# Dilated attention in a decoder step: the statistics exchange moved to GpSimd's DMA queue, scaling of probabilities split from their transposes, and another trace order

## Chip, cores and metric

One core of one Trainium2 chip. The metric is the device time of one execution in microseconds (us), the median of several runs. Engines: PE (TensorE), DVE (VectorE), ACT (ScalarE), POOL (GpSimd) and SP, which here only issues DMAs.

## What is computed

One step of a two-layer decoder trunk for a prompt of 512 tokens and 8 samples of 4 tokens, all fp32: a recurrent block and a ConvFFN, then one shared K/V, then attention with its own queries, then a second ConvFFN. Only the attention is touched by the change. Cut to what matters:

```python
WINDOWS, DILATIONS = (128, 512, 2048), (1, 4, 16)      # three groups of queries, 8 heads of 64

def dilated_band_attn(q, k, v, dilation, span):        # one group; query t reads t, t-d, ..., t-window
    s = jnp.where(valid, einsum(q, k) * HEAD_DIM ** -0.5, -inf)
    m = max(s); p = exp(s - m); den = sum(p)
    return einsum(p, v) / den, m + log(den)

def combine_groups(outs, lses):                        # the three groups of a head are merged
    w = softmax(stack(lses), axis=0)
    return sum(w * stack(outs))
```

The prompt group and the sample group (whose keys are a cache of 256 rows and the 4 new ones) go through the same mathematics and share all weights.

## The kernel before, in words

All tokens are columns: 544 of them (512 prompt, 32 sample) in two halves of 272, features on the 128 partitions. Weights come from memory in units of 128x1024, and each is split by ACT and DVE (L132, L133) into two parts for three matmuls per product. The two FFNs, before and after the attention, take most of the time and are almost all matmuls.

**The attention** is the stretch between `man.close()` (L909) and `man.enter_context` (L1195). Outside it PE's order is that of the text. Inside it the tile framework's planner sets the order on every engine: it goes through the work by the order of the trace (what is written earlier has precedence) and takes what its own model of time holds to be ready. On the chip each engine, and each queue, then runs its list strictly in order. Some things so run earlier than they are written: the mask matmuls of `s_scores` for the first two samples stand between those of two heads.

For each of 8 heads `scores(h)` makes two blocks of scores in PSUM, one for the group of dilation 1 (L932, L937; queries in natural order) and one for the other two groups together (L949, L952; queries ordered by residue modulo 4). DVE takes the negative maximum of each row into `st` (L941, L956), ACT the exponentials into `P0` and `pt` with their sums into `st` (L945, L959), and POOL adds the two groups of `pt` into `P12` (L961). `pt` has two buffers. The P0 and P12 of heads 0 to 3 lie in the buffers that later take sample values; those of heads 4 to 7 use the 8 buffers of split weights.

Since the two blocks have their queries in different orders, the statistics of each must be brought into the order of the other before the groups can be merged. `exchange(half)` (L963) does it for four heads at once, through memory: two stores of 16 KB from `st` to `tok`, one for each block (L968, L969), and two loads from `tok` to `xt` (L970, L971), all four on SP's queue, each load behind the store of the same `tok`. `weights(half)` (L973) turns `st` and `xt` into the factors `sc` in eight small DVE operations and two of ACT (L978 to L987). `p_trans(h)` (L991) scales the head's probabilities by `sc` on DVE (L994, L996, L997), transposes them on PE (L1002, L1007) and moves the result from PSUM to `PT` with ACT (L1003) and DVE (L1008). `p_v(pair)` (L1018) multiplies two heads' `PT` by the values (L1034) and splits the result (L1038, L1039).

The samples run between the heads: `s_scores(b)` (L1062) for each of 8 batches, two at a time in `sample_pair`, in the two single PSUM banks, with keys `ck` loaded on SP's queue (L1048, 512 KB each, four buffers); `s_weights()` (L1076) merges their groups in a chain of small operations and ends with eight DVE scalings of `PS` (L1110); `s_values()` (L1112) transposes them (L1118), sums groups (L1121) and multiplies by the cached values (L1131). After the attention come the output projection (L194 with `OT`, then L1201) and the second FFN.

The order in which all this is written (L1149 to L1188) is in the code below.

Of the kernel before, what the change touches and what calls it, by code (L numbers as in the profile page):

```python
# [45 lines left out]
def trunk_kernel(ctx, tc, wall, xin, par_d, cst_d, msk_d, rope_d, bmask_d, ckT_d, cv_d,  # L46
                 y_d, h_d, conv_d, ffn_d, kT_d, v_d, vs_d):
    nc = tc.nc
    PE, ACT, DVE, POOL, SP = nc.tensor, nc.scalar, nc.vector, nc.gpsimd, nc.sync
# [30 lines left out]
    def big():  # L80
        return psum["pp"].tile([P, 2, 512], F32, name="big", tag="big")

    def bank():
        return psum["aux"].tile([P, 512], F32, name="bank", tag="bank")
# [826 lines left out]
    stat, P0, P12 = {}, {}, {}  # L911

    def own(i):

        return slice(0, 128) if i == 0 else slice(256 * i - 128, 256 * i + 128)
# [9 lines left out]
    def scores(h):  # L925

        c, kz = h // 2, KZ[h % 2][:, h // 2].rearrange("p (r j) -> p r j", r=4)
        half, hl = h // 4, h % 4
        st = stat[half][0]
        ps = big()  # L930
        for i in range(2):
            PE.matmul(ps[:, i, :], lhsT=identb, rhs=mskp[:, 512 * i:512 * i + 512], start=True, stop=True)  # L932
        for i in range(4):
            o = ps[:, i // 2, 256 * (i % 2):256 * (i % 2) + 256]
            for b in range(max(0, i - 1), i + 1):
                n = 128 * (b - i + 1)
                PE.matmul(o[:, n:n + 128].rearrange("p (r j) -> p r j", r=4),  # L937
                          lhsT=QT[0, c // 2][:, c % 2, 128 * i:128 * i + 128], rhs=kz[:, :, 32 * b:32 * b + 32],
                          start=False, stop=True, skip_group_check=True)
        pv_ = ps.rearrange("p x (y k) -> p (x y) k", k=256)  # L940
        DVE.tensor_reduce(st[:, 0, :, hl, 0], pv_, axis=AX.X, op=ALU.max, negate=True)  # L941
        P0[h], P12[h] = head_room(h)
        for i in range(4):
            lo = 128 if i == 0 else 0
            ACT.activation(P0[h][:, own(i)], pv_[:, i, lo:], AF.Exp, bias=st[:, 0, i, hl, 0:1],  # L945
                           accum_out=st[:, 0, i, hl, 1:2])
        ps = big()
        for i in range(2):
            PE.matmul(ps[:, i, :], lhsT=identb, rhs=msk[:, 1024:1536], start=True, stop=True)  # L949
        for r in range(4):  # L950
            for g in (1, 2):
                PE.matmul(ps[:, r // 2, 256 * (r % 2) + 128 * (g - 1):256 * (r % 2) + 128 * g],  # L952
                          lhsT=QT[g, c // 2][:, c % 2, 128 * r:128 * r + 128], rhs=kz[:, r], start=False, stop=True,
                          skip_group_check=True)
        pv_ = ps.rearrange("p x (y k) -> p (x y) k", k=256)
        DVE.tensor_reduce(st[:, 1, :, hl, 0], pv_, axis=AX.X, op=ALU.max, negate=True)  # L956
        pt = tp.tile([P, 4, 2, 128], F32, name="pt", tag="pt", bufs=2)
        for r in range(4):
            ACT.activation(pt[:, r].rearrange("p g k -> p (g k)"), pv_[:, r], AF.Exp, bias=st[:, 1, r, hl, 0:1],  # L959
                           accum_out=st[:, 1, r, hl, 1:2])  # L960
        POOL.tensor_tensor(P12[h], pt[:, :, 0], pt[:, :, 1], op=ALU.add)  # L961

    def exchange(half):  # L963
        st, xt, sc = stat[half]
        tok = [dram.tile([4, P, 8], F32, name=f"tok{half}{i}") for i in range(2)]

        flat = [t.rearrange("i p z -> (i p z)").rearrange("(j r z) -> j r z", r=4, z=8) for t in tok]
        SP.dma_start(tok[0].rearrange("i p z -> p i z"), st[:, 0].rearrange("p i e z -> p i (e z)"))  # L968
        SP.dma_start(flat[1], st[:, 1].rearrange("p r e z -> p r (e z)"))  # L969
        SP.dma_start(xt[:, 1].rearrange("p r e z -> p r (e z)"), flat[0])  # L970
        SP.dma_start(xt[:, 0].rearrange("p i e z -> p i (e z)"), tok[1].rearrange("i p z -> p i z"))  # L971

    def weights(half):  # L973
        st, xt, sc = stat[half]
        m1, m2, d1, d2 = st[:, :, :, :, 0], xt[:, :, :, :, 0], st[:, :, :, :, 1], xt[:, :, :, :, 1]
        t = [tp.tile([P, 2, 4, 4], F32, name=f"wt{i}", tag=f"wt{i}", bufs=1) for i in range(3)]

        DVE.tensor_tensor(t[0], m1, m2, op=ALU.min)  # L978
        DVE.tensor_tensor(t[1], t[0], m1, op=ALU.subtract)
        DVE.tensor_tensor(t[2], t[0], m2, op=ALU.subtract)  # L980
        ACT.activation(t[1], t[1], AF.Exp)
        ACT.activation(t[2], t[2], AF.Exp)
        DVE.tensor_tensor(t[0], t[1], d1, op=ALU.mult)
        DVE.tensor_tensor(t[2], t[2], d2, op=ALU.mult)
        DVE.tensor_tensor(t[0], t[0], t[2], op=ALU.add)
        DVE.reciprocal(t[0], t[0])
        DVE.tensor_tensor(sc, t[1], t[0], op=ALU.mult)  # L987

    PT = {}

    def p_trans(h, half, hl):  # L991
        sc = stat[half][2]
        p0, p12 = P0.pop(h), P12.pop(h)
        DVE.tensor_scalar(p0[:, own(0)], p0[:, own(0)], sc[:, 0, 0, hl:hl + 1], None, op0=ALU.mult)  # L994
        rest = p0[:, 128:896].rearrange("p (i k) -> p i k", k=256)
        DVE.tensor_tensor(rest, rest, sc[:, 0, 1:4, hl:hl + 1].to_broadcast([P, 3, 256]), op=ALU.mult)  # L996
        DVE.tensor_tensor(p12, p12, sc[:, 1, :, hl:hl + 1].to_broadcast([P, 4, 128]), op=ALU.mult)  # L997
        pt = tp.tile([P, 11, 128], F32, name="PT", tag="PT", bufs=2)
        PT[h] = pt
        ps = big()  # L1000
        for n in range(7):
            PE.transpose(ps[:, n // 4, 128 * (n % 4):128 * (n % 4) + 128], p0[:, 128 * n:128 * n + 128], ident)  # L1002
        ACT.activation(pt[:, 0:7].rearrange("p n q -> p (n q)"),  # L1003
                       ps.rearrange("p x y -> p (x y)")[:, 0:896], AF.Copy)
        ps = bank()
        for r in range(4):
            PE.transpose(ps[:, 128 * r:128 * r + 128], p12[:, r], ident)  # L1007
        DVE.tensor_copy(pt[:, 7:11].rearrange("p n q -> p (n q)"), ps)  # L1008
# [67 lines left out]
    def s_weights():  # L1076

        ps = bank()
        for i in range(2):
            PE.transpose(ps[0:8, 128 * i:128 * i + 128], sden[:, i], ident)  # L1080
        t = tp.tile([8, 2, 128], F32, name="sw", tag="pt", bufs=2)
        w = tp.tile([8, 128], F32, name="sw2")
        m = tp.tile([8, 3, 8, 4], F32, name="sw3")
        DVE.tensor_copy(t.rearrange("b i r -> b (i r)"), ps[0:8, 0:256])

        def by_group(x):
            return x.rearrange("b (h g s) -> b g h s", g=4, s=4)

        mm, dd, ww = by_group(t[:, 0]), by_group(t[:, 1]), by_group(w)
        POOL.memset(w, 0.0)  # L1090
        lo, acc, tt = (tp.tile([8, 8, 4], F32, name=f"sl{i}") for i in range(3))

        DVE.tensor_tensor(lo, mm[:, 0], mm[:, 1], op=ALU.min)
        DVE.tensor_tensor(lo, lo, mm[:, 2], op=ALU.min)
        for g in range(3):
            DVE.tensor_tensor(m[:, g], lo, mm[:, g], op=ALU.subtract)
        ACT.activation(m, m, AF.Exp)
        for g in range(3):
            DVE.tensor_tensor(acc if g == 0 else tt, m[:, g], dd[:, g], op=ALU.mult)
            if g:  # L1100
                DVE.tensor_tensor(acc, acc, tt, op=ALU.add)
        DVE.reciprocal(acc, acc)
        for g in range(3):
            DVE.tensor_tensor(ww[:, g], m[:, g], acc, op=ALU.mult)
        ps = bank()
        PE.transpose(ps[:, 0:8], w, ident[0:8, 0:8])
        wr = tp.tile([P, 8], F32, name="wr")
        DVE.tensor_copy(wr, ps[:, 0:8])
        for b in range(8):
            DVE.tensor_scalar(PS[:, b], PS[:, b], wr[:, b:b + 1], None, op0=ALU.mult)  # L1110

# [43 lines left out]
    def sample_pair(i):  # L1155
        for b in (2 * i, 2 * i + 1):
            s_scores(b)
            if b + 4 < 8:
                load_ck(b + 4)

    scores(4)
    sample_pair(0)
    weights(0)
    scores(5)
    sample_pair(1)
    for h in (0, 1):
        p_trans(h, 0, h)
        scores(6 + h)
    exchange(1)
    p_v(0)  # L1170
    sample_pair(2)
    p_trans(2, 0, 2)
    sample_pair(3)
    p_trans(3, 0, 3)
    for b in range(8):
        load_cv(b)
    s_weights()
    weights(1)
    p_v(1)
    p_trans(4, 1, 0)  # L1180
    p_trans(5, 1, 1)
    s_values()
    p_v(2)
    p_trans(6, 1, 2)
    p_trans(7, 1, 3)
    p_v(3)
    nxt["stop"] = firsts[1]
    conv_more(WBUFS - 2)  # L1188
# [195 lines left out]
```

## Time and profile before

| | us |
|---|---|
| median of 3 runs | 1279.61 (1278.06 to 1280.74) |
| the profiled execution, its own time | 1277.12 |
| its span, first to last instruction | 1275.2 |
| PE busy in the span | 1229.0 (96%) |
| DVE busy | 1035.0 (81%) |
| ACT busy | 701.4 (55%) |
| POOL busy | 175.6 (14%) |
| the attention, 739.6 to 834.9 | 95.3 |

The shares are over the whole span, where PE is almost never idle; the attention is the one longer stretch where it is, and where the clock that TensorE is granted falls. Times inside the span are given from its first instruction. A "releaser" in a row is the instruction that ended the engine's wait.

### The profile page before, as it was taken

What the parts mean: (1) busy time and instruction counts of PE and PEld (TensorE: products, weight loads), DVE (VectorE), ACT (ScalarE), POOL (GpSimd) and SP (SyncE); (2) the same over time, 40 slices, a digit from 0 to 9 for tenths busy, and PEclk for the clock granted to TensorE, in tenths of its full rate; (3) what the DMA queues carried; (4) which work ended last, traced back from release to release, by engine and by line L of the source; (5) the groups of instructions that cost most, each with busy time, mean ns of one, the idle gap of its engine ahead of it and who ended that gap; (6) DMA issues with size and microseconds to landing.
All of it is one profiled execution on the core that took longest, in us unless ns stands there. A gap on an engine that the chain in (4) does not pass through costs nothing.

```text
span 1275.2 us, 23856 instructions
## 1 busy us (share of the span) xinstructions
PE 1229.0 (96%) x9665; PEld 1197.0 (94%) x9665; DVE 1035.0 (81%) x1634; ACT 701.4 (55%) x1203; POOL 175.6 (14%) x235
## 2 busy tenths in 40 slices
PE   7999998999999999999999998798999999999998
PEld 7999998999999999999999886588999999999998
DVE  8985769998989797967878746789898989797963
ACT  5778646655555554545555365256655555454641
POOL 2464332000000000005113421032000000000000
PEclk9999999999999999999999998899899999999999
DMA  5232221233323232323245374321233323232422
GB/s 211 84 110 92 85 84 46 83 104 100 100 84 103 97 100 83 124 85 135 86 145 149 94 228 135 117 67 37 80 100 102 112 85 100 84 115 84 123 69 85
DMA packets 42909, 130.96 MB, mean 103 GB/s; under 512 B 7952, under 2 KB 8464, under 8 KB 42672
## 3 DMA queue, kind: packets, MB, share of 16 engines
q1 hardware_dynamic: 42800, 129.44, 32.1%
q8 instruction: 76, 1.25, 0.4%
q14 instruction: 33, 0.27, 0.1%
HBM read 121.03 MB, written 8.39 MB: 101 GB/s over the span
## 4 chain that ended last, share of the span: by engine, by line
PE 82%; DVE 8%; ACT 5%; issue 2%; POOL 1%; DMA 0%; SPq 0%; POOLq 0%; DVEq 0%; ACTq 0%
PE big L194 37%; PE bank L497 36%; PE big L881 2%; PE big L952 1%; DVE w L133 1%; PE big L937 1%; PE big L1034 1%; DVE hl L255 1%; ACT w L132 1%; PE big L1002 1%; ACT KZ L843 1%; PE big L760 0%; PE bank L1131 0%; DMA raw<-in_wall 0%; PE bank L881 0%
## 5 line engine op out<-in xcount | busy, mean ns | idle before, releaser
L194 PE MATMUL big<-HH,w 128*128 128x272 f32 x1536 | 259.3, 289 | 0.5 <-ACT cr L613 0.5
L194 PE MATMUL big<-hh,w 128*128 128x272 f32 x1280 | 219.9, 290 | 7.4 <-ACT hh L254 6.0
L497 PE MATMUL bank<-hh,w 128*128 128x272 f32 x1056 | 221.2, 289 | 0.0
L194 PEld LDWEIGHTS big<-HH,w 128*128 128x128 f32 x1536 | 218.0, 188 | 2.2 <-DVE X L638 1.3
L194 PEld LDWEIGHTS big<-hh,w 128*128 128x128 f32 x1280 | 184.1, 190 | 8.1 <-ACT hh L254 6.0
L497 PEld LDWEIGHTS bank<-hh,w 128*128 128x128 f32 x1056 | 175.0, 190 | 0.0
L194 PE MATMUL big<-HL,w 128*128 128x272 f32 x768 | 159.2, 288 | 0.8 <-DVE HL L307 0.8
L132 ACT ACTIVATE w<-raw 128x1024 fp32r<-128x1024 f32 (+1 forms) x111 | 113.4, 1029 | 76.6 <-PE big L194 59.0
L497 PE MATMUL bank<-t12h,w 128*128 128x272 f32 x704 | 142.4, 292 | 10.6 <-ACT snap L502 10.6
L497 PE MATMUL bank<-hl,w 128*128 128x272 f32 x528 | 152.3, 289 | 0.0
L133 DVE TENSOR_TENSOR w<-raw,w 128x1024 fp32r<-128x1024 f32 (+1 forms) x111 | 141.4, 1277 | 10.7 <-ACT w L132 5.8
L497 PE MATMUL bank<-t34h,w 128*128 128x272 f32 x704 | 146.2, 287 | 0.0
L194 PE MATMUL big<-hl,w 128*128 128x272 f32 x640 | 134.0, 291 | 1.9 <-DVE hl L255 1.9
L164 ACT ACTIVATE w<-sum 128x1024 fp32r<-128x1024 f32 x88 | 93.1, 1058 | 71.9 <-PE big L194 35.3
L497 PEld LDWEIGHTS bank<-t12h,w 128*128 128x128 f32 x704 | 115.3, 192 | 11.0 <-ACT snap L502 11.0
L194 PEld LDWEIGHTS big<-HL,w 128*128 128x128 f32 x768 | 120.6, 188 | 1.2 <-DVE HL L307 1.2
L502 ACT ACTIVATE snap<-bank 128x272 f32<-128x272 f32 x176 | 69.4, 395 | 89.5 <-PE bank L497 84.4
L165 DVE TENSOR_TENSOR w<-sum,w 128x1024 fp32r<-128x1024 f32 x88 | 107.5, 1222 | 13.3 <-PE bank L497 9.7
L497 PEld LDWEIGHTS bank<-t34h,w 128*128 128x128 f32 x704 | 115.7, 188 | 0.0
L194 PEld LDWEIGHTS big<-hl,w 128*128 128x128 f32 x640 | 101.3, 190 | 2.9 <-DVE hl L255 2.9
L497 PE MATMUL bank<-t12l,w 128*128 128x272 f32 x352 | 102.2, 290 | 0.0
L497 PE MATMUL bank<-t34l,w 128*128 128x272 f32 x352 | 101.1, 287 | 0.0
(277 smaller groups left out, 2278.1 us busy)
## 6 DMA issues: line engine op xcount, KB each, us to landing
raw<-in_wall SPq DMA_DIRECT2D x193, 512.0 KB, 3.5
ck<-in_ckT SPq DMA_DIRECT2D x8, 512.0 KB, 7.3
X<-in_xin SPq DMA_DIRECT2D x8, 272.0 KB, 6.1
out_y<-X SPq DMA_DIRECT2D x8, 272.0 KB, 2.1
cv<-in_cv SPq DMA_DIRECT2D x8, 256.0 KB, 4.4
cvt<-in_cv SPq DMA_DIRECT2D x4, 512.0 KB, 5.0
raw<-in_wall SPq DMA_DIRECT2D x6, 256.0 KB, 5.2
out_kT<-KT SPq DMA_DIRECT2D x2, 544.0 KB, 4.6
```

Of the source, the lines that this page charges most:

```text
L132: ACT.activation(hi[:, c0:c1], st, AF.Copy)
L133: DVE.tensor_tensor(lo[:, c0:c1], st, hi[:, c0:c1].bitcast(F32), op=ALU.subtract)
L164: ACT.activation(hi, flat, AF.Copy)
L165: DVE.tensor_tensor(lo, flat, hi.bitcast(F32), op=ALU.subtract)
L194: PE.matmul(ps[:, h, :T], lhsT=w[wi], rhs=x[xi][:, h, :], start=first and wi == 0 and xi == 0, stop=last and wi == 1)
L255: DVE.scalar_tensor_tensor(lo, X[k], g, hi.bitcast(F32), op0=ALU.mult, op1=ALU.subtract)
L497: PE.matmul(dst, lhsT=w, rhs=form(n, k, xi), start=first and k == 0 and wi == 0 and xi == 0, stop=k == 3 and wi == 1, skip_group_check=True)
L502: ACT.activation(t, src, AF.Copy)
L843: ACT.activation(KZ[a][rows, 2 * i + cc].rearrange("p (r j) -> p r j", r=4), residues(KT[i][rows, cc, 0:512]), AF.Copy)
L881: PE.matmul(o, lhsT=l, rhs=w[wi][:, 512 * kk:512 * kk + 512], start=k == 0 and wi == 0 and xi == 0, stop=k == KC - 1 and wi == 1)
L937: PE.matmul(o[:, n:n + 128].rearrange("p (r j) -> p r j", r=4), lhsT=QT[0, c // 2][:, c % 2, 128 * i:128 * i + 128], rhs=kz[:, :, 32 * b:3 ...
L952: PE.matmul(ps[:, r // 2, 256 * (r % 2) + 128 * (g - 1):256 * (r % 2) + 128 * g], lhsT=QT[g, c // 2][:, c % 2, 128 * r:128 * r + 128], rhs ...
```

## The change

It has three parts, all in the attention. The four DMAs of `exchange` are issued by POOL in place of SP. `p_trans` is cut in two: `p_scale(h)` holds the three DVE scalings, `p_trans(h)` the transposes and copies; likewise the eight scalings at the end of `s_weights` become `s_scale`. And the order of the trace is new: `scores(5)` and then `weights(0)` and `p_scale(0)` stand before `sample_pair(1)`; for heads 0 and 1 the next head's scaling follows the transposes, ahead of the next scores; `weights(1)` and `p_scale(4)` stand before `s_weights`, `s_scale` after the transposes of head 5, and `s_values` after `p_v(2)` and the scaling of head 7. No arithmetic is added or taken away.

```diff
     def exchange(half):
...
-        SP.dma_start(tok[0].rearrange("i p z -> p i z"), st[:, 0].rearrange("p i e z -> p i (e z)"))
-        SP.dma_start(flat[1], st[:, 1].rearrange("p r e z -> p r (e z)"))
-        SP.dma_start(xt[:, 1].rearrange("p r e z -> p r (e z)"), flat[0])
-        SP.dma_start(xt[:, 0].rearrange("p i e z -> p i (e z)"), tok[1].rearrange("i p z -> p i z"))
+        POOL.dma_start(tok[0].rearrange("i p z -> p i z"), st[:, 0].rearrange("p i e z -> p i (e z)"))
+        POOL.dma_start(flat[1], st[:, 1].rearrange("p r e z -> p r (e z)"))
+        POOL.dma_start(xt[:, 1].rearrange("p r e z -> p r (e z)"), flat[0])
+        POOL.dma_start(xt[:, 0].rearrange("p i e z -> p i (e z)"), tok[1].rearrange("i p z -> p i z"))
...
-    def p_trans(h, half, hl):
-        sc = stat[half][2]
-        p0, p12 = P0.pop(h), P12.pop(h)
+    def p_scale(h, half, hl):
+        sc, p0, p12 = stat[half][2], P0[h], P12[h]
         DVE.tensor_scalar(p0[:, own(0)], p0[:, own(0)], sc[:, 0, 0, hl:hl + 1], None, op0=ALU.mult)
         rest = p0[:, 128:896].rearrange("p (i k) -> p i k", k=256)
         DVE.tensor_tensor(rest, rest, sc[:, 0, 1:4, hl:hl + 1].to_broadcast([P, 3, 256]), op=ALU.mult)
         DVE.tensor_tensor(p12, p12, sc[:, 1, :, hl:hl + 1].to_broadcast([P, 4, 128]), op=ALU.mult)
+
+    def p_trans(h):
+        p0, p12 = P0.pop(h), P12.pop(h)
...
         DVE.tensor_copy(wr, ps[:, 0:8])
+        return wr
+
+    def s_scale(wr):
         for b in range(8):
             DVE.tensor_scalar(PS[:, b], PS[:, b], wr[:, b:b + 1], None, op0=ALU.mult)
...
     scores(4)
     sample_pair(0)
+    scores(5)
     weights(0)
-    scores(5)
+    p_scale(0, 0, 0)
     sample_pair(1)
     for h in (0, 1):
-        p_trans(h, 0, h)
+        p_trans(h)
+        p_scale(h + 1, 0, h + 1)
         scores(6 + h)
     exchange(1)
     p_v(0)
     sample_pair(2)
-    p_trans(2, 0, 2)
+    p_trans(2)
+    p_scale(3, 0, 3)
     sample_pair(3)
-    p_trans(3, 0, 3)
+    p_trans(3)
     for b in range(8):
         load_cv(b)
-    s_weights()
     weights(1)
+    p_scale(4, 1, 0)
+    wr = s_weights()
+    p_scale(5, 1, 1)
     p_v(1)
-    p_trans(4, 1, 0)
-    p_trans(5, 1, 1)
+    p_trans(4)
+    p_trans(5)
+    s_scale(wr)
+    p_scale(6, 1, 2)
+    p_v(2)
+    p_scale(7, 1, 3)
     s_values()
-    p_v(2)
-    p_trans(6, 1, 2)
-    p_trans(7, 1, 3)
+    p_trans(6)
+    p_trans(7)
     p_v(3)
```

## Rows read from the trace of the kernel before

**Rows 1.** Windows: the attention cut by stage (first row: scores of heads 0 to 5; then the first gap, the slow restart, scores 6 and 7, the work up to the second gap, the second gap, and the samples' values), and all that follows it. Columns: the stretch and its length in us; busy us and instructions of PE, weight loads, DVE, ACT, POOL; granted clock of TensorE as a share of full speed; busy share of the DMA engines; GB/s.

```profile
739.60:767.30 27.70, 26.95 (x241) 24.47 (x241) 14.61 (x13) 21.62 (x91) 6.53 (x7) 1.00 0.71 234
767.30:776.00 8.70, 3.11 (x42) 1.57 (x38) 3.67 (x15) 4.31 (x18) 1.27 (x1) 0.62 0.75 216
776.00:779.20 3.20, 3.20 (x14) 2.62 (x15) 3.20 (x7) 0.63 (x1) 0.00 (x0) 0.50 0.20 81
779.20:788.70 9.50, 9.50 (x80) 8.91 (x79) 7.90 (x10) 5.60 (x23) 1.27 (x1) 0.98 0.35 112
788.70:801.00 12.30, 12.28 (x185) 9.47 (x184) 6.70 (x22) 7.99 (x27) 1.28 (x1) 1.00 0.55 173
801.00:813.00 12.00, 7.81 (x34) 6.08 (x36) 10.71 (x33) 4.32 (x5) 0.00 (x0) 0.61 0.27 93
813.00:822.50 9.50, 7.88 (x79) 5.88 (x76) 8.37 (x21) 2.46 (x3) 0.00 (x0) 0.96 0.43 122
834.90:1275.20 440.30, 429.57 (x3389) 427.85 (x3388) 367.52 (x573) 227.26 (x388) 19.44 (x18) 0.99 0.28 90
```

**Rows 2.** Timeline of the first gap: start us, us, engine, line, operation, out<-in, shapes, count, and in brackets the idle time before it with its releaser.

```profile
770.03 0.37 PE L1064 MATMUL bank<-msk,identb 128*128 128x256 bf16 x1 [2.70 <-ACT PS L1074]
...
773.09 0.46 DVE L1073 TENSOR_REDUCE sden<-bank 128x1 f32<-128x288 f32 x1 [1.02 <-PE bank L1071]
773.47 0.18 DVE L978 TENSOR_TENSOR wt<-st,xt 128x32 f32<-128x32 f32 x1
...
775.28 0.19 DVE L987 TENSOR_TENSOR sc<-wt,wt 128x32 f32<-128x32 f32 x1
775.58 0.29 DVE L994 TENSOR_SCALAR P<-P,sc 128x128 f32<-128x128 f32 x1
...
775.92 0.48 PE L1002 MATMUL big<-cst,P 128*128 128x128 f32 x1 [2.90 <-DVE P L994]
```

**Rows 3.** Timeline of SP's queue around the two exchanges: start us, time of the issue, line, DMA, count.

```profile
758.72 0.38 SPq L968 DMA_DIRECT2D tok<-st  x1
761.11 0.33 SPq L969 DMA_DIRECT2D tok<-st  x1
766.92 0.33 SPq L1048 DMA_DIRECT2D ck<-in_ckT  x1
767.34 0.38 SPq L970 DMA_DIRECT2D xt<-tok  x1
767.78 0.42 SPq L971 DMA_DIRECT2D xt<-tok  x1
...
792.07 0.32 SPq L969 DMA_DIRECT2D tok<-st  x1
792.48 0.88 SPq L1053 DMA_DIRECT2D cvt<-in_cv  x2
793.52 0.38 SPq L971 DMA_DIRECT2D xt<-tok  x1
```

**Rows 4.** DMA issues, each from a window that holds the issue alone: the second store and the loads of the first exchange (the last of these three rows is the median of its two loads), then the second store and the last load of the second exchange. Columns: DMA, queue, count, KB each, us from issue to landing.

```profile
tok<-st SPq DMA_DIRECT2D x1, 16.0 KB, 3.1
...
xt<-tok SPq DMA_DIRECT2D x1, 16.0 KB, 3.1
...
xt<-tok SPq DMA_DIRECT2D x2, 16.0 KB, 3.3
...
tok<-st SPq DMA_DIRECT2D x1, 16.0 KB, 1.4
...
xt<-tok SPq DMA_DIRECT2D x1, 16.0 KB, 5.1
```

**Rows 5.** Timeline of POOL in the attention: the addition of heads 3, 4 and 7, columns as in the timeline above.

```profile
761.16 1.26 POOL L961 TENSOR_TENSOR P<-pt 128x512 f32<-128x512 f32 x1 [2.94 <-ACT pt L959]
765.37 1.27 POOL L961 TENSOR_TENSOR P12w<-pt 128x512 f32<-128x512 f32 x1 [2.94 <-ACT pt L959]
...
792.12 1.28 POOL L961 TENSOR_TENSOR P12w<-pt 128x512 f32<-128x512 f32 x1 [3.88 <-ACT pt L959]
```

**Rows 6.** Timeline of DVE in the second gap, columns as above.

```profile
799.52 0.17 DVE L978 TENSOR_TENSOR wt<-st,xt 128x32 f32<-128x32 f32 x1
799.62 0.18 DVE L1093 TENSOR_TENSOR sl<-sw 8x32 f32<-8x32 f32 x1
...
801.64 0.69 DVE L1039 TENSOR_TENSOR OT<-big,OT 128x512 fp32r<-128x512 f32 x1 [0.17 <-ACT OT L1038]
...
802.56 0.28 DVE L994 TENSOR_SCALAR P0w<-P0w,sc 128x128 f32<-128x128 f32 x1
...
805.38 2.31 DVE L1110 TENSOR_SCALAR PS<-PS,wr 128x288 f32<-128x288 f32 x8
...
808.22 0.94 DVE L996 TENSOR_TENSOR P0w<-P0w,sc 128x768 f32<-128x768 f32 x1
```

**Rows 7.** Timeline of the stage after the attention: one DVE operation alone, and the same operation beside one of POOL, columns as above.

```profile
839.69 0.79 DVE L255 SCALAR_TENSOR_TENSOR hl<-X,par,hh 128x544 fp32r<-128x544 f32 x1 [0.82 <-ACT hh L254]
...
850.39 1.37 POOL L274 TENSOR_TENSOR ss<-ss,sqx 128x544 f32<-128x544 f32 x1 [0.93 <-ACT sqx L268]
850.47 1.88 DVE L255 SCALAR_TENSOR_TENSOR hl<-X,par,hh 128x544 fp32r<-128x544 f32 x1
```

## The prediction

> **What bounds the kernel now.** I read the windows by stage first. After the attention PE is busy 429.57 of 440.30 us at a clock of 0.99 [rows 1]: nothing there waits on what the change touches, so a microsecond taken from the attention should come off the end. Inside it, the first 27.7 us (scores of heads 0 to 5) are PE at full clock and so is the stretch from 788.7 to 801. Two stretches are not [rows 1]. From 767.3 to 776.0 PE is busy 3.11 of 8.70 us, at 0.62, and restarts at half clock: 776.0 to 779.2 is busy throughout at 0.50 (1.2 GHz, the lower of its two levels; 1.00 is 2.4). From 801 to 813 it is busy 7.81 of 12.00 at 0.61. I call them the first and the second gap. The second has a different bound from the first: DVE is busy there 10.71 of 12.00 us, and 8.37 of the 9.50 behind it, where in the first it is busy only 3.67 of 8.70.
>
> Then I read the timeline of the first gap [rows 2]. PE waits twice: 2.70 us for a PSUM bank, freed by ACT's exponential of a sample, and 2.90 us for the first scaled probabilities. Behind the second wait stands a DVE chain: sample maxima at 773.09, `weights(0)` from 773.47, `sc` at 775.28, scaling at 775.58, transposes at 775.92. From L978 to the scaling it takes 775.58 - 773.47 = 2.1 us. Was `weights(0)` held by its data or by DVE's list? SP's queue and the landings tell [rows 3, 4]: the stores went out at 758.72 and 761.11, the second landed 3.1 us later, at 764.2; but the loads stood behind a `ck` load that could only go at 766.92, so they were issued at 767.34 and 767.78. One took 3.1 us, and with a median of 3.3 the other took 3.5: the data were there at 771.3. The remaining 2.2 us, to 773.47, are DVE's list: the maxima of samples 2 and 3 came first.
>
> In the second exchange nothing blocks the queue. Its second store goes at 792.07, lands in 1.4, the load goes at 793.52 and takes 5.1 us behind two 512 KB loads of `cvt`: 798.6 [rows 3, 4]. `weights(1)` starts at 799.52 [rows 6].
>
> **Part 1, the exchange on POOL.** Arithmetic is the same; four SP issues of 0.32 to 0.42 us [rows 3] per exchange go, and four POOL issues come. No DMA of the trace before is issued by POOL, so a leg (issue to landing of one) is bounded by rows. Below: SP's fastest, 1.4 us [rows 4]; a leg may come out shorter than now, since it no longer shares a queue with the large loads. Above: SP's slowest, 5.1 us [rows 4], and one POOL instruction's length, 1.3 us [rows 5], for the issue: 6.4. I take L = 3.5, nearest to the legs of the first exchange (3.1, 3.1, 3.5), which ran beside other loads as these will.
>
> The exchange's end is two legs in a row, second store and its load. On POOL the second store stands behind the addition of the same exchange's last head, written before it and ready at the same time: 761.16 + 1.26 = 762.4, and 792.12 + 1.28 = 793.4 [rows 5]. So the data land at 762.4 + 2L = 769.4 in the first (771.3 now), and at 793.4 + 2L = 800.4 in the second (799.52 is when it is used now). The first gets earlier, the second later by 2L - 6.1 = 0.9 us.
>
> Behind a waiting load on POOL stand the additions of later heads. Head 4's is ready at 765.37 [rows 5] and could wait for the last load's store. `pt` has two buffers, so ACT would miss it only two heads on, in scores 6 after 779.2 [rows 1]: more than 13 us of slack. I cost it at nothing; a wait beyond that would stop ACT and then PE by the excess. SP loses a blocker; it bounds nothing here.
>
> **Part 2, order at the first gap.** `weights(0)` and `p_scale(0)` now precede the maxima of samples 2 and 3. With data at 769.4 the first scaled block is there at 769.4 + 2.1 + 0.3 = 771.8. PE meanwhile runs the second sample pair, from 770.03 as now, since its bank is freed by ACT, which the change does not touch; it ends at 773.0. The transposes follow with no wait: 2.9 us gained. PE then runs without a break from 770.03. Now it restarts at 775.92 and is granted 0.50 until 779.2, which costs 3.2 x (1 - 0.50) = 1.6 us [rows 1]; I take 1.1 of it as saved, as the sample pair is then the slow restart. First gap: -2.9 - 1.1 = -4.0. What is late next there is the bank, 2.7 us, which stays. The scalings one head ahead gain nothing by themselves: PE is busy 9.50 of 9.50 us in the scores behind it [rows 1].
>
> **Part 3, order at the second gap.** Now the chain of `weights(1)` is interleaved with that of `s_weights`, and an `OT` operation of 0.69 us gets in: from 799.52 to the scaling at 802.56 it takes 3.0 us against 2.1 in the first half [rows 2, 6]. Head 5's scaling stands behind eight sample scalings of 2.31 us and ends at 809.16 [rows 6]. With the new order the first costs 0.9 less and the second 2.3 less for PE's next transposes. But both move DVE's work and remove none, and DVE is busy 10.71 + 8.37 = 19.08 of 21.5 us here [rows 1]: only the 2.4 us of idle time can be closed. I take -2.0, with 0 as one end (DVE ends its list when it did) and -4 as the other (PE's slow clock is recovered too, 0.61 over 7.81 us).
>
> **Sum.** -4.0 + 0.9 - 2.0 = -5.1 us: the profiled execution of 1277.12 goes to 1272.0. It lies 2.5 below the median of the runs; the forecast is made for the median: 1279.61 - 5.1 = 1274.5.
>
> On one point the Trainium skill speaks against the change. The rows first: the same DVE operation takes 0.79 us alone and 1.88 beside one of POOL's [rows 7], so the two engines hold each other up. SBUF — State Buffer, section "SBUF: two separate sides", says that POOL's DMAs have descriptors written by GpSimd, which a DVE operation in a two-port mode locks out, so that a DMA of about 620 ns takes about 3100. No row here shows such a DMA; by that figure each leg would be some 2.5 us longer, an estimate, and with L = 6.0 the sum would be a loss. The Trainium skill's page DMA: Bandwidth & Descriptors, section "Anatomy of one DMA — SWDGE (gpsimd) path", has it the other way, about 2.0 us fixed and little for 16 KB: with L = 2.0 the second exchange would be 2.1 us early and the sum near -8, an estimate as well.
>
> **Rivals.**
> (a) Slower: POOL's legs are long, by its own issue or by DVE's work on the ports. Both exchanges pay twice per leg. The first gap's gain lasts while 762.4 + 2L is well before 773.47 and is a loss above L = 5.5; the second pays 2L - 6.1. At L = 4.9 the second pays 3.7 against about 1.7 and 2.0 gained: the point from which it decides. At L = 6.0 the first loses 0.9, the second 5.9, and 2.0 is gained: +4.8, 1284.4. For it: POOL's operations are stretched in rows 7's manner, and the second exchange has little slack, 799.52 - 798.6. Against it: around 761 to 770 DVE is half idle.
> (b) No change: L near 4.4, and DVE's list behind the second gap ends when it did. The first gap gives -2.2 - 0.9, the second +2.7 and 0: -0.4, about 1279. For it: DVE's 19.08 of 21.5 us.
> (c) More: L about 2.5, the own queue passing the large loads. The second exchange is 1.1 early, the order is worth its full 4, the first gap gives 5: -10, about 1269.5. For it: legs of 1.4 us without traffic [rows 4].
> (d) The planner doesn't give the order that is written, for instance puts the sample maxima ahead of `weights(0)` again. Then only the data's 0 to 2 us remain; with the second exchange +0.9 and order -1 that is within 1 us of now, and is counted with (b). Behind the attention its lists on DVE and ACT may also fall otherwise; PE's idle time there is 10.7 us of 440.3 [rows 1], and I allow 1 to 2 us either way.
>
> **How the numbers follow.** Chances: forecast (-3 to -8) 0.48, (c) 0.11, (b) and (d) 0.21, (a) 0.20. About 0.2%, 2.6 us, is what a measurement of this kernel can tell from no change. Faster by more: 0.57, from the forecast and (c) less a small edge; within: 0.23; slower by more: 0.20. The range runs from (c) with planner's luck, 1268, to (a) at its price, 1284.5; the likeliest case's own range is 1271.5 to 1277.
>
> **What would show it.** Right: in the first gap PE's 2.90 us before L1002 gone, and the transposes directly behind the second sample pair; `sc` of the first half before 773; legs of POOL of about 3.5 us; L996 of head 5 before the eight L1110; the clock at 1.0 some 4 us earlier; scores 7 ended by about 785. Wrong: POOL's DMAs landing after 5 us or more, `weights(1)` starting more than 3 us later against the end of scores 7 than now (799.52 - 788.7 = 10.8), DVE without idle time from `weights(1)` to the last L1121 and that stretch as long as before, or new idle time of PE after the attention.

## The result, and the profile after

The changed kernel takes 1285.59 us (median of 6 runs, 1282.94 to 1287.68) against 1279.60 for the kernel before (6 runs): a ratio of 1.0053, 95% interval 1.0042 to 1.0065. It is slower by some 6 us where 5.1 us less were forecast, and it lies above the range. The profiled execution takes 1284.72 us with a span of 1282.6; before it was 1277.12 and 1275.2, so the pair of traces below differs by 7.4 to 7.6 us.

The windows by stage of the changed kernel, cut as before [rows 1] in front and at its own waits behind (from 792.40: the second exchange, the second gap in two rows, the samples' values, and what follows the attention; columns as in rows 1):

```profile
767.30:776.00 8.70, 2.72 (x26) 1.70 (x23) 5.93 (x14) 3.35 (x14) 1.26 (x1) 0.81 0.33 121
776.00:779.20 3.20, 3.20 (x30) 2.38 (x26) 1.52 (x3) 1.45 (x3) 0.00 (x0) 0.50 0.52 160
...
792.40:804.40 12.00, 8.06 (x120) 5.71 (x110) 3.02 (x6) 4.46 (x11) 3.11 (x4) 0.96 0.81 265
804.40:817.90 13.50, 11.00 (x86) 8.69 (x88) 12.59 (x43) 3.90 (x7) 0.00 (x0) 0.78 0.01 3
817.90:827.36 9.46, 5.59 (x37) 3.40 (x38) 9.18 (x25) 3.29 (x4) 0.00 (x0) 0.82 0.30 91
827.36:841.44 14.08, 12.45 (x107) 5.49 (x107) 5.76 (x11) 2.27 (x4) 0.00 (x0) 0.88 0.17 52
841.44:1282.60 441.16, 429.67 (x3389) 427.95 (x3388) 366.95 (x573) 227.29 (x388) 19.42 (x18) 0.99 0.28 90
```

The first gap is as wide as it was: PE is busy 2.72 of 8.70 us (3.11 before), although DVE now has 5.93 us of work in it (3.67 before). From 792.40 to 804.40 PE loses 3.94 us, where before it was busy without a break up to 801 [rows 1], and in the row behind, DVE is busy 12.59 of 13.50 us. What follows the attention is not the cause: PE is busy there as long as before (429.67 against 429.57).

For a comparison over all kernels I take four marks from the timelines of PE and DVE, in us after the first score matmul of the attention (L932, at 739.61 before and 739.75 after): the first transposes of scaled probabilities; the end of scores 7; from there to the first L978 of `weights(1)`; and from that to the first matmul on `OT`.

| | first transposes | end of scores 7 | to `weights(1)` | to `OT` | span |
|---|---|---|---|---|---|
| before | 36.3 | 49.15 | 10.76 | 35.32 | 1275.2 |
| after | 33.9 | 49.36 | 15.31 | 36.95 | 1282.6 |

So in this pair of traces the first half gave nothing (+0.2), the second exchange cost 4.55, the stretch behind it 1.63, and 0.9 came behind the attention: 7.3.

**The first gap.** The timelines of PE, DVE and ACT there, after (the third and later columns as in rows 2):

```profile
772.93 0.37 PE L1066 MATMUL bank<-msk,identb 128*128 128x256 bf16 x1 [5.45 <-ACT PS L1076]
...
773.64 0.47 PE L1004 MATMUL big<-cst,P 128*128 128x128 f32 x1 [0.31 <-DVE P L993]
```

```profile
767.15 0.19 DVE L978 TENSOR_TENSOR wt<-st,xt 128x32 f32<-128x32 f32 x1 [1.75 <-DMA xt<-tok]
767.26 1.22 DVE L956 TENSOR_REDUCE st<-big 128x4 f32<-128x1024 f32 x1
768.39 0.18 DVE L979 TENSOR_TENSOR wt<-wt,st 128x32 f32<-128x32 f32 x1
...
770.65 1.24 DVE L983 TENSOR_TENSOR wt<-wt,st 128x32 f32<-128x32 f32 x1 [1.98 <-ACT wt L981]
771.81 0.44 DVE L1075 TENSOR_REDUCE sden<-bank 128x1 f32<-128x288 f32 x1
...
773.30 0.28 DVE L993 TENSOR_SCALAR P<-P,sc 128x128 f32<-128x128 f32 x1
```

```profile
770.38 0.24 ACT L981 ACTIVATE wt<-wt 128x32 f32<-128x32 f32 x1
...
772.28 0.50 ACT L1076 ACTIVATE PS<-bank,sden 128x288 f32<-128x288 f32 x1 [1.55 <-DVE sden L1075]
```

The wait before the scaled probabilities is down from 2.90 to 0.31 us, and the wait for the bank is up from 2.70 to 5.45 [rows 2]: 5.60 became 5.76. The data were there at 767.15. But L956, head 5's maxima, stands behind L978, ACT takes the two exponentials of `weights(0)` (L981) only after those of head 5, at 770.38, and the sample maxima, which free the bank, stand behind L983 of `weights(0)`: 771.81. L983 itself took 1.24 us beside POOL's addition for head 5 (770.58 to 771.84), where the same instruction of `weights(1)` takes 0.18 (805.46).

**The second exchange.** The queues of POOL and SP after, and the chain that ended last (start us, us, what):

```profile
762.52 0.57 POOL L969 DMA_DIRECT2D tok<-st  x1
763.09 0.56 POOL L970 DMA_DIRECT2D xt<-tok  x1
764.79 0.76 POOL L971 DMA_DIRECT2D xt<-tok  x1 [1.15 <-DMA tok<-st]
...
792.48 1.27 POOL L961 TENSOR_TENSOR P12w<-pt 128x512 f32<-128x512 f32 x1 [1.20 <-ACT pt L959]
793.71 0.57 POOL L969 DMA_DIRECT2D tok<-st  x1
794.28 0.55 POOL L970 DMA_DIRECT2D xt<-tok  x1
797.72 0.76 POOL L971 DMA_DIRECT2D xt<-tok  x1 [2.89 <-DMA tok<-st]
```

```profile
792.52 1.89 SPq L1055 DMA_DIRECT2D cvt<-in_cv  x2
794.58 0.33 SPq L1062 DMA_DIRECT2D cv<-in_cv  x1
796.72 1.19 SPq L1055 DMA_DIRECT2D cvt<-in_cv  x2
798.00 1.94 SPq L1062 DMA_DIRECT2D cv<-in_cv  x3
```

```profile
792.48 1.23 POOL P12w L961
793.71 3.73 DMA tok<-st
797.44 0.28 issue
797.72 6.58 DMA xt<-tok
804.42 0.20 DVE wt L978
```

How that reaches PE, in the timelines of DVE and PE after:

```profile
804.42 0.19 DVE L978 TENSOR_TENSOR wt<-st,xt 128x32 f32<-128x32 f32 x1 [6.28 <-DMA xt<-tok]
...
804.86 0.68 DVE L1010 COPY PT<-bank 128x512 f32<-128x512 f32 x1
```

```profile
805.60 1.97 PE L1036 MATMUL big<-PT,VP 128*64 128x128 f32 x14 [5.14 <-DVE PT L1010]
```

In the first exchange the legs are 2.3, 2.0, 2.0 and 2.2 us, and the data land 4.3 us earlier than before (767.0 against 771.3). In the second the two legs in a row are 3.73 and 6.58 us, and they are on the critical chain: DVE stands still for 6.28 us in front of L978, and the copy to `PT` behind it in DVE's list (L1010) keeps PE waiting for 5.14. On SP the second store had gone out at 792.07, ahead of the first `cvt` load at 792.48, and landed in 1.4 us [rows 3, 4]. On POOL nothing holds that order: the store goes at 793.71, when the loads of `cvt` have been under way for a microsecond. This is a reading of one pair of traces; the experiments try it.

### The profile page after: what moved, and what is told of

Same layout as the page of the kernel before. It is cut to its first block, busy times and chain, and to the rows that moved or that the text cites. A ratio compares the mean times of both kernels' runs of the same rounds, so it can differ in the third digit from the quotient of the medians.

```text
span 1282.6 us, 23859 instructions
## 1 busy us (share of the span) xinstructions
PE 1230.2 (96%) x9659; PEld 1196.3 (93%) x9665; DVE 1036.0 (81%) x1634; ACT 701.4 (55%) x1203; POOL 180.4 (14%) x243
## 4 chain that ended last, share of the span: by engine, by line
PE 80%; DVE 8%; ACT 6%; issue 2%; DMA 2%; POOL 1%; SPq 0%; POOLq 0%; DVEq 0%; ACTq 0%
PE big L194 37%; PE bank L497 36%; PE big L881 2%; DVE w L133 1%; ACT w L132 1%; DVE hl L255 1%; DMA xt<-tok 1%; PE bank L1136 1%; PE big L937 1%; PE big L952 1%; ACT KZ L843 1%; DMA X<-in_xin 0%; POOL ss L274 0%; PE big L760 0%; PE big L1036 0%
## 5 line engine op out<-in xcount | busy, mean ns | idle before, releaser
L497 PEld LDWEIGHTS bank<-t12h,w 128*128 128x128 f32 x704 | 115.3, 191 | 10.4 <-ACT snap L502 10.4
```

Source lines behind the costliest of these rows:

```text
L497: PE.matmul(dst, lhsT=w, rhs=form(n, k, xi), start=first and k == 0 and wi == 0 and xi == 0, stop=k == 3 and wi == 1, skip_group_check=True)
```

## The experiments

Ratios are against the kernel before on the same chip, with their 95% interval. Three theories stood to be told apart: the second exchange on POOL is the loss, the new order is, or both; and for the exchange, the large loads beside it against POOL and DVE in each other's way.

**Four mixtures of queue and order.** The first is the changed kernel with the exchange on SP, the second the kernel before with it on POOL, the third and fourth the changed kernel with one exchange on POOL alone.

```diff
# e1, from the changed kernel (four DMAs; e2 is the reverse, from the kernel before)
-        POOL.dma_start(tok[0].rearrange(...
+        SP.dma_start(tok[0].rearrange(...
# e3, from the changed kernel (four DMAs; e4 has SP if half == 0 else POOL)
+        Q = POOL if half == 0 else SP
-        POOL.dma_start(tok[0].rearrange(...
+        Q.dma_start(tok[0].rearrange(...
```

The new order alone, on SP:

> The changed kernel with the exchange back on SP: split and order alone. Theory A (the last leg of the second exchange, late on POOL, starts weights(1) 4.9 us later than before and costs just that): weights(1) starts within 1 us of 799.5 and the time is 1285.6 - 4.9 = 1280.7. Theory B (the new order costs, by DVE's list and PE's slow clock at its end; the queue is harmless): about 1285, with the stretch from weights(1) to the end of the attention 37 us as in the changed kernel, against 35.4 before.

Measured: 1280.42, ratio 1.0016 (1.0006 to 1.0027). To `weights(1)` 10.29 us, from there to `OT` 37.01 (35.32 before). The order itself costs, behind the second exchange.

POOL alone, in the old order:

> The kernel before with the exchange on POOL and nothing else. Theory A: 1279.6 + 4.9 = 1284.5, with the last leg of the second exchange at 5 us or more and weights(1) at about 804. Theory B: 1279 or less, since the first exchange lands some 4 us earlier.

Measured: 1281.74, 1.0029 (1.0020 to 1.0038). To `weights(1)` 15.97, legs of 4.71 and 6.27 us; to `OT` 34.27.

The first exchange on POOL, new order:

> The changed kernel with only the first exchange on POOL, the second on SP. Theory A: 1280.7, as with both on SP, if the first gap gains nothing from data that land 4 us earlier; if it gains the forecast 4 us after all, 1277. Theory B: 1285.

Measured: 1277.68, 0.9991 (0.9981 to 1.0001). On SP again, the second exchange's legs are 1.41 and 4.51 us, and `weights(1)` comes after 9.37. PE waits 5.55 us for the bank in the first gap, as in the changed kernel.

The second exchange on POOL, new order:

> The changed kernel with only the second exchange on POOL, the first on SP. Theory A: 1285 to 1286, as the changed kernel. Theory B: 1285 as well, but with weights(1) at 800 and the loss behind it. A third reading, that POOL's exchange costs in the first gap (PE's bank wait of 5.4 us in place of 2.7), expects about 1283.

Measured: 1285.09, 1.0053 (1.0037 to 1.0068), as the changed kernel; legs of 5.24 and 5.44.

What follows: the POOL queue is worth -2.7 us at the first exchange (1277.68 against 1280.42) and +4.7 at the second (1285.09 against 1280.42). With +2.0 of the order that makes +4.0, by medians of about a microsecond's uncertainty each; the changed kernel is at +6.0, so the parts don't add up. One reason shows: beside a second exchange on POOL, the first one on POOL gained nothing (1.0053 in the changed kernel, 1.0053 in e4), so the -2.7 can't be counted there. The order alone (+2.0, e1) and the queue alone (+3.3, e2: 1281.74 against 1278.41) make +5.3.

**The old order with the first exchange on POOL alone** (`Q = POOL if half == 0 else SP` in the kernel before):

> The kernel before, its order kept, with only the first exchange on POOL and the second on SP. If the first exchange's early data are worth what the run with POOL alone showed (scores 7 end 1.8 us earlier) and the second's landing on SP is as before, weights(1) starts some 1.8 us earlier and the time is 1278.4 - 1.8 = 1276.6 (before at 1278.4 on this kind of chip). If the whole gain needs the new order as well: 1278 to 1279.

Measured: 1276.44, 0.9980 (0.9972 to 0.9989). PE's two waits in the first gap became one:

```profile
770.85 0.45 PE L1003 MATMUL big<-cst,P 128*128 128x128 f32 x1 [3.84 <-DVE P L995]
```

3.84 in place of 5.60, 1.8 us less. The first transposes start 5.2 us earlier (31.1 after the first score matmul against 36.3), but scores 7 end only 1.0 us earlier: the second sample pair, which PE did in its gap before, is now behind the transposes.

**The changed kernel with the loads held.** A POOL write into each buffer, which needs the second exchange's data, stands before the loads of `cvt` and the late ones of `cv`, so that these start when the statistics have landed:

```diff
# e6, from the changed kernel (the same before the cv loads of b > 5)
+            POOL.tensor_copy(t[:, 0, 0:1], stat[1][1][:, 0, 0, 0, 0:1])
             SP.dma_start(t.rearrange("p c e -> p (c e)"), cv_d[b])
```

> The changed kernel, both exchanges on POOL, with the loads of cv that ran beside the second exchange held back until it has landed (POOL writes one element of each of their tiles from xt first; eight copies of one column). Theory A1 (the 512 and 256 KB loads in flight make the legs long): the second exchange's last legs fall from 3.7 and 6.6 us to 2.0 to 2.3, as in the first, weights(1) starts some 5 to 6 us after the end of the additions of head 7, and the time is 1285.6 - 5 = about 1280. Theory A2 (a POOL DMA is slow there for another reason, DVE's operations on the shared ports or POOL's own work): the legs stay at 4 us or more and the time at 1285.

Measured: 1277.73, 0.9993 (0.9984 to 1.0002), some 8 us below the changed kernel, and `weights(1)` after 8.95 us. Its DMA issues, window 790 to 806 (columns as in rows 4, each the median of two), and the windows over the two legs in it (first) and over the two legs in the changed kernel (second and third):

```profile
tok<-st POOLq DMA_DIRECT2D x2, 16.0 KB, 1.9
xt<-tok POOLq DMA_DIRECT2D x2, 16.0 KB, 2.1
```

```profile
794.41:798.73 4.32, 4.32 (x63) 3.22 (x61) 1.83 (x4) 2.80 (x6) 1.89 (x4) 1.00 0.09 11
```

```profile
793.71:797.44 3.73, 3.73 (x55) 2.77 (x53) 1.48 (x3) 2.33 (x5) 1.12 (x3) 1.00 0.84 269
797.72:804.42 6.70, 2.74 (x34) 1.77 (x30) 0.42 (x1) 0.77 (x4) 0.76 (x1) 0.93 0.89 300
```

With the DMA engines at 0.09 a leg on POOL takes 1.7 to 2.2 us, at 0.84 and 0.89 it takes 3.7 and 6.6. DVE speaks against the other theory: it is busier beside the short legs (1.83 of 4.32) than beside the longest (0.42 of 6.70). So it is the large loads.

**The fastest mixture of these parts**: old order, first exchange on POOL, second on SP, the large loads issued on SP behind its last DMA (`with tc.issue_after(last[1]):` around the loads of `cvt`, and of `cv` for b > 5; those of b = 4 and 5 behind the last `ck` load).

> The order of before, first exchange on POOL, second on SP with the loads of cv of samples 0 to 3 and 6, 7 issued behind its last load. Theory A1: that last leg falls from 4.5 to 5.1 us to 1.4 to 2.0, weights(1) can start 2 to 3 us earlier, 1276.6 - 2 = 1274.6; if DVE's and PE's lists hold weights(1) instead, no gain, 1276.6. Theory A2 expects the leg as it was.

Measured: 1275.55, 0.9982 (0.9973 to 0.9992); the two legs in a row of the second exchange are 1.4 and 1.9 us. Though they sum to 3.3 against 6.5 before, `weights(1)` is only 1.2 us earlier (9.54): DVE's list and PE's work in front of it are next. Against e5, 0.9 us are gained, less than the intervals can tell. In e5 the legs were 4.7 and 1.8, for there the planner put one `cvt` load ahead of the store on SP's own queue (L1054, L970), and two others behind the exchange's last load (L972):

```profile
791.07 0.33 SPq L1054 DMA_DIRECT2D cvt<-in_cv  x1
791.50 0.37 SPq L970 DMA_DIRECT2D tok<-st  x1
...
796.22 0.37 SPq L972 DMA_DIRECT2D xt<-tok  x1
796.68 0.93 SPq L1054 DMA_DIRECT2D cvt<-in_cv  x2
```

**The store ahead of the addition**: the changed kernel, with head 7's POOL addition put behind the exchange.

```diff
# e8
-        POOL.tensor_tensor(P12[h], pt[:, :, 0], pt[:, :, 1], op=ALU.add)
+        add = lambda: POOL.tensor_tensor(P12[h], pt[:, :, 0], pt[:, :, 1], op=ALU.add)
+        if h < 7: add()
+        else: late.append(add)
...
     exchange(1)
+    late.pop()()
```

> The changed kernel with POOL's addition of head 7 written behind the exchange, so that the second store need not stand behind it. If the 1.3 us of that addition, which let two large loads of cvt go out first, are what makes the second exchange late, its two legs become 2 and about 5 us, weights(1) starts some 3 us earlier and the time is about 1282.5. If only the 1.3 us themselves count: 1284.3. If the legs stay as they are whatever the start: 1285.6.

Measured: 1285.01, 1.0051 (1.0038 to 1.0064). The store goes 1.0 us earlier, at 792.69, still behind the first `cvt` load (792.52), takes 4.90, and the load goes at 797.88, as late as ever, and takes 5.8. A start 1.0 us earlier is worth nothing here. A store ahead of the large loads on POOL's queue was not tried, since this one still came behind the first of them.

**The order, one half at a time**, all exchanges on SP. e9 is the changed kernel with the second half's order of before, e10 that with the first half's:

```diff
# e9, from the changed kernel (beside SP in the exchange)
+    s_scale(s_weights())
     weights(1)
+    p_v(1)
     p_scale(4, 1, 0)
-    wr = s_weights()
...
-    s_scale(wr)
...
# e10, from the changed kernel (beside SP in the exchange)
-    scores(5)
     weights(0)
-    p_scale(0, 0, 0)
+    scores(5)
     sample_pair(1)
     for h in (0, 1):
+        p_scale(h, 0, h)
         p_trans(h)
-        p_scale(h + 1, 0, h + 1)
...
```

> All exchanges on SP. The first half's steps stand in the changed kernel's order (scaled probabilities and statistics as there, up to the transposes of head 3), the second half's in the order of before. Theory, the second half's order is what costs the 1.6 us that the run with the changed order on SP alone showed between the second weights and the outputs: here that stretch stays at 35.3 us as before, the first stretch at 33.7, and the time at about 1278.8, no change. Rival, the first half's order costs it (DVE enters the second half with its work in another sequence): the stretch is 37.0 us and the time about 1280.4.

Measured: 1277.88, 0.9998 (0.9987 to 1.0009), to `OT` 35.29.

> All exchanges on SP, the mirror of the run beside it: the first half in the order of before, the second half's weights, scaled probabilities and transposes in the changed kernel's order. Theory, the second half's order costs: the stretch from the second weights to the outputs is 37.0 us and the time about 1280.4 (ratio 1.0013). Rival, the first half's order costs: 35.3 us and about 1278.8.

Measured: 1280.33, 1.0018 (1.0009 to 1.0028). The second half's order is what costs. (Its stretch to `OT` is 41.2 us in a profiled execution that took 2.4 us more than the median; the excess is PE at half clock: the two groups of 16 value matmuls take 3.64 us each, 1.93 and 1.92 in e9.) The row that moved is `wr`, the sample weights, on which the eight sample scalings wait; `weights(1)` (first row) and `wr` of e9, then of e10:

```profile
799.76 0.17 DVE L978 TENSOR_TENSOR wt<-st,xt 128x32 f32<-128x32 f32 x1
...
805.35 0.17 DVE L1110 COPY wr<-bank 128x8 f32<-128x8 f32 x1 [0.30 <-PE bank L1108]
805.63 2.32 DVE L1115 TENSOR_SCALAR PS<-PS,wr 128x288 f32<-128x288 f32 x8
```

```profile
800.23 0.18 DVE L978 TENSOR_TENSOR wt<-st,xt 128x32 f32<-128x32 f32 x1
...
808.96 0.17 DVE L1110 COPY wr<-bank 128x8 f32<-128x8 f32 x1 [0.45 <-PE bank L1108]
810.00 0.69 DVE L1010 COPY PT<-bank 128x512 f32<-128x512 f32 x1 [0.88 <-PE bank L1009]
...
811.97 0.69 DVE L1010 COPY PT<-bank 128x512 f32<-128x512 f32 x1 [1.00 <-PE bank L1009]
812.58 2.03 DVE L1115 TENSOR_SCALAR PS<-PS,wr 128x288 f32<-128x288 f32 x7
```

`wr` comes 5.59 us after `weights(1)` in e9 and 8.73 in e10; the scalings end at 807.95 and at 814.61, and in e10 DVE stands idle three times in front of them (0.45 + 0.88 + 1.00).

**DVE's list, made shorter.** e11 is e7 with the eight sample scalings on ACT, e12 is e6 with the same edit:

```diff
-            DVE.tensor_scalar(PS[:, b], PS[:, b], wr[:, b:b + 1], None, op0=ALU.mult)
+            ACT.activation(PS[:, b], PS[:, b], AF.Copy, scale=wr[:, b:b + 1])
```

> The order of before, the first exchange on POOL, the second on SP with the big context loads held until its data have landed (the fastest kernel so far, 1275.55), and here the scaling of the eight score tiles of the second half is done by ACT in place of DVE. Theory, DVE's list of work bounds the stretch from the second weights to the outputs (12.59 of 13.50 us busy in the changed kernel): some 2.3 us come off DVE, the stretch falls from 34.2 to about 32, and the time to about 1273.3. Rival, the chain through the scaled probabilities, their transposes and the matmuls bounds it: the stretch stays at 34.2 and the time at 1275.5; if ACT becomes the bound instead, it grows to about 36 and the time to 1277.5.

Measured: 1271.46, 0.9943 (0.9931 to 0.9956): the fastest kernel here, 7 us below the kernel before on its chip. To `OT` 30.96 us. ACT takes 3.50 us for the eight, in its idle time:

```profile
804.02 3.50 ACT L1116 ACTIVATE PS<-PS,wr 128x288 f32<-128x288 f32 x8
```

> The changed kernel (new order in both halves, both exchanges on POOL) with the big context loads held until the second exchange has landed, and with the eight sample scalings of the second half done by ACT. Without the last it took 1277.73 us, ratio 0.9993. Theory, the new order costs because DVE waits for the sample weights with the eight scalings (2.31 us) still on its list: with these on ACT the order costs nothing, and the time comes to about 1272, as the run of the old order with the same edit (1271.46), the stretch from the second weights to the outputs to about 32 us. Rival, the order delays the sample scalings whoever does them, and the transposes behind them wait: about 1275, the stretch at 34 us or more.

Measured: 1274.22, 0.9966 (0.9954 to 0.9979), to `OT` 34.55. DVE's 2.3 us are worth 3.5 here (from 1277.73), but the rival was right on the order: it still costs 2.8 against e11, with the scalings off DVE. `wr` comes 10.33 us after `weights(1)` (808.50 - 798.17), 5.04 in e11 (802.87 - 797.83). (e11 also has its second exchange on SP, but `weights(1)` comes as long after scores 7 in both, 9.55 us in e11 and 9.45 here.) ACT waits for `wr`:

```profile
808.68 3.52 ACT L1118 ACTIVATE PS<-PS,wr 128x288 f32<-128x288 f32 x8 [3.11 <-DVE wr L1113]
```

## Why the prediction was wrong

**What bounds the kernel.** The two gaps were the right places, and the stages behind the attention stayed as they were within 0.9 us. But each of the three terms of the sum failed: -4.0, +0.9 and -2.0 were forecast, +0.2, +4.55 and +1.6 stand in the trace.

**Part 1, the first exchange.** The step held, on the good side: legs of 2.0 to 2.3 us where 3.5 were taken, data at 767.0 where 769.4 were computed. The head 4 addition behind the waiting load cost nothing, as said (765.57, against 765.37 [rows 5]).

**Part 1, the second exchange: the step that failed first.** "The second later by 2L - 6.1 = 0.9 us", with one L = 3.5 for both exchanges. It measured 4.55 against the end of scores 7: legs of 3.73 and 6.58, that is L = 5.2, and 2 x 5.2 - 6.1 = 4.3. So the formula was right and L was mis-sized, and not by POOL: I took the shorter queue as a gain ("no longer shares a queue with the large loads") and did not see that the shared queue is what put the 1.4 us store in front of the first large load [rows 3]. A leg has no length of its own here. On POOL it is 1.7 to 2.3 us with the DMA engines at 0.12 or less, and 3.7 to 6.6 beside the `cvt` and `cv` loads; on SP the two legs in a row of the second exchange are 1.4 to 2.7 clear of them and 4.0 to 5.1 beside them. The two exchanges needed two values, and the nearest row for the second was its own load, 5.1 us [rows 4], which I kept only as the upper bound. Nor did the three legs from which I took 3.5 all run beside other loads: during the store of 3.1 us (761.11 to 764.20) the engines were at 0.06.

Rival (a) gave this outcome and nearly the size (1284.4), with a point of decision at L = 4.9 that the second exchange did pass. Its two mechanisms are not what happened: POOL's issue took 0.55 to 0.93 us, e6 shows DVE's work beside short legs, and only the second exchange paid. By the rule of the Trainium skill that I put beside it (SBUF — State Buffer, section "SBUF: two separate sides") a leg beside a DVE operation in a two-port mode is longer by some 2.5 us, an estimate. The legs of the first exchange and of e6, 1.7 to 2.3 us with DVE busy 0.42 to 0.46 of the time, don't show it; whether any of DVE's operations there was in such a mode, no row tells. The Trainium skill's page DMA: Bandwidth & Descriptors, section "Anatomy of one DMA — SWDGE (gpsimd) path", has about 2.0 us fixed. These legs agree with it; the section says nothing of the load beside them.

**Part 2, the first gap: -4.0 forecast, +0.2 in the trace.** The 2.90 us did go, and "what is late next there is the bank, 2.7 us, which stays" is the sentence that failed: the bank became later by as much, 5.45. The samples' maxima and exponentials, which free it, share DVE and ACT with the chain that I put in front of them; I had written that the change doesn't touch ACT. Rival (d) had seen that the planner's list may differ from the written order, but named the other direction (sample maxima first). What became of the earlier data was measured in other kernels: -2.7 in the new order (e3 against e1), -2.4 in the old (e5). The new order of the first half by itself is worth nothing (e9, 0.9998). The gain of clock, 1.1 us, did not come in the changed kernel's trace: behind the long wait 776.0 to 779.2 is at 0.50 as before, and the clock is back at 1.00 39.8 us after the first score matmul, 40.0 before. That is partly this trace: e3, e6, e8 and e12 have the first half in the same order with its exchange on POOL, and there the clock is back at 37.0 to 38.3 and scores 7 end at 47.98 to 48.75, 0.4 to 1.2 us earlier than before.

**Part 3, the second gap: -2.0 forecast, +1.6 in the profile, +2.0 by e1.** I costed the order by the transposes of heads 4 and 5, which do come earlier against `weights(1)`. What ends the stretch is another chain, the samples': `s_weights`, `wr`, the eight scalings, their transposes, reductions and value matmuls. The order puts the scalings of heads 4 to 6 into that chain's way and delays `wr` against `weights(1)` by 3.1 us (e10 against e9) and 5.3 (e12 against e11). "DVE ends its list when it did" was no end on the bad side: an order that fills DVE with the wrong work lets it run dry behind. That DVE's list bounds the stretch is supported by e11, where 2.3 us less on it give 3.3 in the stretch and 4.1 in the time; more than was taken off, but the clock differs too (1.00 in the 13.5 us from `weights(1)`, 0.87 in e7).

**Order or clock.** The order costs in two ways, and the traces tell them apart by the first 16 value matmuls. From the end of these to `OT` every kernel but e10 takes 10.4 us. In the new order they start later behind `weights(1)` than in the old order with the same queues: by 1.7 us in e1 (24.66 against 22.97 before), 1.5 in e3 (against e5) and 1.0 in the changed kernel (22.94 against 21.91 in e2); by 1.6 in e12 against e11. And in two of these four traces they run at half clock. In e1 they take 1.92 us, as before, in the changed kernel 3.58:

```profile
825.52 1.92 PE L1136 MATMUL bank<-cvt,pst 128*32 128x512 f32 x16 [1.00 <-PE bank L1123]
```

```profile
827.36 3.58 PE L1136 MATMUL bank<-cvt,pst 128*32 128x512 f32 x16 [0.44 <-PE bank L1123]
```

So in e1 none of the 1.7 us lies in these matmuls' clock. In the changed kernel they start as long after the late `weights(1)` as before (22.94 and 22.97), and their half clock makes up the 1.63. In e12 they take 3.91.

**What stays open.** Why they are at half clock in one kernel and not in the next, what is left of the excess of the changed kernel over its parts (6.0 against 5.3, within the uncertainty), and the 0.9 us behind the attention. Also the legs on SP in the first exchange: its second store took 1.4 us in e1 and 3.1 to 3.6 before, in e4 and in e10, where the DMA engines were at 0.06 to 0.08, so the large loads don't explain that.

## What to carry to other kernels

Moving a small DMA to a queue of its own also takes away the order that the old queue gave it: ask which large transfers were behind it there, and hold them back if they now go first (e6 gained 8 us over the changed kernel by that alone). A shared queue alone doesn't fix it either: in e5 the planner put a large load ahead. Where an engine is nearly full, an order is judged by the chain that ends the stretch, here the samples' weights, not by the wait that one sees on PE; and taking work off that engine (e11) gave more than any order of it. Before a wait is counted as gained, the next wait on the same engine must be followed to its own producers, since these may stand in the list behind the very work that was moved forward.

## What the hardware showed

- A DMA of 16 KB on POOL's queue took 1.7 to 2.3 us with the DMA engines at a share of 0.09 to 0.12, 3.7 at 0.84 and 6.6 at 0.89, beside loads of 256 and 512 KB on SP's queue. A separate queue was no protection.
- The issue itself keeps POOL 0.55 to 0.93 us, against 0.32 to 0.42 on SP [rows 3].
- A DVE operation of 128x32 (L983) took 1.24 us beside an addition of POOL (1.26 us), and 0.18 without one.
- The same eight scalings of 128x288 take 2.31 us on DVE [rows 6] and 3.50 on ACT.
